# A modulation vector's columns: weighted sums on three engines, or one-column products on TensorE

## The chip, the core and the metric

The kernel runs on one core of a Trainium2 chip. Time is device time in microseconds (us) of one execution. Below, a "column" is one value for each of the 128 partitions.

## What is computed

Two transformer-like blocks follow one another on x of 1024 tokens by 1024 channels. Only the beginning of the first block matters here:

```python
mod = (jax.nn.silu(c) @ w_ada + b_ada)[:, None, :]      # c: (1, 1024), w_ada: (1024, 3072)
shift, scale, gate = jnp.split(mod, 3, axis=-1)
h = rms_norm(x, norm_g) * (1.0 + scale) + shift
... = jnp.split(h @ w_in, IN_OFFSETS, axis=-1)
```

All else (four attention-like branches on slices of `h @ w_in`, a merge, an output product scaled by `gate`, and the whole second block with its MLP) follows it. `p @ w_ple_proj` of the second block depends on inputs alone and is computed at the beginning as well.

## The kernel before, in words

Channels lie on partitions, in 8 pieces of 128 (KC = 8). Large products are made in three matmuls of 512 columns each, from a high and a low half of either operand (`mm3`, lines 229 to 231). A copy to the high half is line 147 (ScalarE) or 149 (VectorE); the subtraction that gives the low half is line 155 (GpSimd) or 157 (VectorE). Transposes are line 276.

The kernel is written in a framework that orders the instructions of each engine when it is compiled: by a priority, taken from the order of the program, and by a simulation of when operands are there. `stream(_T["STA"], -30000000)` gives the instructions traced inside it a priority ahead of all others, so that they are placed as soon as the simulation has them ready. `tc.issue_after(ins)` keeps instructions behind `ins` on the same engine. Each engine then runs its list strictly in that order.

The first stage, up to about 115 us, does this in the order of the program:

- It loads the rows of p and the weights of its projection, then the first half of x (512 tokens). All loads of this stage go through `load`, which puts them on SyncE's queue one behind the other.
- `proj(0)`, `x_norm(0)` and `proj(1)`: two halves of the projection of p (48 matmuls of 512 columns each), and between them the scaling and transposes of the first half of x.
- Four rounds over kp. Each makes two calls of `ada_cols` (one for 256 columns of the shift, one for 256 of the scale), then `x_mod(0, [kp])`, the modulation of two channel pieces: ScalarE makes the high half (line 412), VectorE the full value (line 413), VectorE or GpSimd the low half. Then come the first products with two pieces of K for four outputs (`first_products`, lines 506 to 508, 24 matmuls of 512 columns a round), which collect in four PSUM banks over all rounds.
- After that the second half of x is scaled, transposed and modulated (`x_norm(1)`), and the products of branch d go on. Then come sums for the gate (`ada_gate`), which have the same line numbers 455 and 458 but the tile name blk, and lie outside the question.

One call of `ada_cols` before: the 1024 by 256 weights come in two transfers of 512 KB (tile wada, eight buffers, 16 transfers in all). The 256 columns of eight pieces of K are multiplied by the piece's silu value (`sc`, one value a partition) and added up, elementwise: pieces 2, 3, 5, 6 and 7 on VectorE (one multiplication, line 455, four multiply-adds, line 458), pieces 0, 1 and 4 on ScalarE (line 451) with two additions on GpSimd (line 453). That leaves two tiles of 128 by 256 (adau). For each of its two outputs TensorE then adds these up over the partitions: the tile's 128 columns are loaded as weights, and a single column of ones is the moving operand (line 470), accumulated over the two tiles. A float32 product is two instructions of each kind in the trace, so 32 products show as 64. Lines 472 and 474 add the bias and form the scale on VectorE.

In the last round, 18 of the 24 products of the third round (outputs 1 to 3) are held behind the last column product by `issue_after`.

Of the kernel before, what the change touches and what calls it, by code (L numbers as in the profile page):

```python
# [9 lines left out]
F32 = mybir.dt.float32  # L10
F32R = mybir.dt.float32r
AF = mybir.ActivationFunctionType
ALU = mybir.AluOpType
# [4 lines left out]
P = 128  # L18
# [3 lines left out]
KC = D // P  # L22
# [54 lines left out]
def hybrid_then_mix_kernel(ctx: ExitStack, tc, I, c1, c2, out, dbg=None, upto=99):  # L77
    nc = tc.nc
    ve, ac, po, pe, sy = nc.vector, nc.scalar, nc.gpsimd, nc.tensor, nc.sync
# [9 lines left out]
    def nm(s):  # L89
        uid[0] += 1  # L90
        return f"{s}_{uid[0]}"

    def blk(dt=F32, shape=(P, 1024)):
        return main.tile(list(shape), dt, name=nm("blk"), tag="blk", bufs=NBLK)
# [10 lines left out]
    def mmb():  # L105
        return bank("mm", _T["MM"])
# [7 lines left out]
    def obk():  # L114
        return bank("o", _T["OB"])
# [87 lines left out]
    def kview(ap):  # L203
        return ap.rearrange("(k p) n -> p k n", p=P)
# [115 lines left out]
    start = ctx.enter_context(ExitStack())  # L320
# [6 lines left out]
    def load(dst, src):  # L327
        if prev[0] is None:
            d = sy.dma_start(dst, src)
        else:  # L330
            with tc.issue_after(prev[0].ins):
                d = sy.dma_start(dst, src)
        prev[0] = d
        return d
# [13 lines left out]
    def proj(half, early=False):  # L348
        if half not in pin:
            proj_load(half, sy.dma_start)  # L350
        b = pin[half]
        pT = A(2)
        pT.alloc(half, 0)
        for k in range(2):
            tp = trb()
            for q in range(4):
                transpose(tp[:, q * P:(q + 1) * P], b[:, q, k * P:(k + 1) * P], ident)
            copy(pT.hi(k, half), tp[:], "a")
            sub_lo(pT.lo(k, half), tp[:], pT.hi(k, half))
        for t in range(4 * half, 4 * half + 4):  # L360
            if early:
                proj_rows[t] = blk()
            for n in range(2):
                cs = slice(n * 512, (n + 1) * 512)
                m = mmb()
                gemm_N(m[:], pT, t, wproj[0], n * 512, n * 512 + 512)
                if early:
                    copy(proj_rows[t][:, cs], m[:], pick("pe", _T["PSE"]), 0.5)
                else:
                    o = tmp("acc", 512)  # L370
                    copy(o[:], m[:], "a", 0.5)
                    sy.dma_start(proj_d[t][:, cs], o[:])

    w_ada = kview(I["w_ada"][0])
# [9 lines left out]
    def x_norm(half):  # L384

        for t in range(4 * half, 4 * half + 4):
            xt = xin[t]
            ss = small(1)
            scr = cur[0].tile([P, 1024], F32, name=nm("scr"), tag="scr", bufs=1)
            sumsq(ss[:], xt[:], scr[:])  # L390
            r = small(1)
            rstd_of(r[:], ss[:], D, 1e-6)
            ve.tensor_scalar_mul(xt[:], xt[:], r[:, 0:1])
        for kp in range(4):
            xT[half, kp] = blk(F32, (P, 2, 512))
            if half:
                hT.alloc(half, kp)
            for j in range(2):
                k = 2 * kp + j
                tp = trb()  # L400
                for q in range(4):
                    transpose(tp[:, q * P:(q + 1) * P], xin[4 * half + q][:, k * P:(k + 1) * P], ident)
                if half:
                    x_mod1(half, kp, j, tp[:])
                else:
                    copy(xT[half, kp][:, j, :], tp[:], "a")
# [22 lines left out]
    sc = main.tile([P, 8], F32, name="sc", tag="sc", bufs=1)  # L429
# [4 lines left out]
    ones = main.tile([P, 1], F32, name="ones", tag="ones", bufs=1)  # L434
    ve.memset(ones[:], 1.0)
    aps = obk()
    mod = main.tile([P, 24], F32, name="mod", tag="mod", bufs=1)

    def ada(c0, n, new_u, new_w, dma, side=(), new_t=None):

        u, u2 = new_u(), side and new_u()
        per = 1024 // n
        fresh = True
        for k in range(KC):
            if k % per == 0:
                w = new_w()
                dma(w[:], w_ada[:, k:k + per, c0:c0 + n])
            wk = w[:, k % per, :]
            if k in side:
                t = u2 if k == min(side) else new_t()  # L450
                ac.activation(t, wk, AF.Copy, scale=sc[:, k:k + 1])
                if k > min(side):
                    po.tensor_tensor(u2, u2, t, op=ALU.add)
            elif fresh:
                ve.tensor_scalar_mul(u, wk, sc[:, k:k + 1])
                fresh = False
            else:
                ve.scalar_tensor_tensor(out=u, in0=wk, scalar=sc[:, k:k + 1], in1=u, op0=ALU.mult, op1=ALU.add)
        return [u, u2] if side else [u]

    def st_tile(tag, bufs, shape):
        return lambda: cur[0].tile([P] + shape, F32, name=nm(tag), tag=tag, bufs=bufs)[:]

    def ada_cols(c0):

        us = ada(c0, 256, st_tile("adau", 6, [256]), st_tile("wada", _T["WB"], [4, 256]), load, _T["PEA"], st_tile("adat", 2, [256]))
        c = slice(c0 // P, c0 // P + 2)
        for m in range(2):
            for j, u in enumerate(us):
                last = pe.matmul(aps[:, c.start + m:c.start + m + 1], u[:, m * P:(m + 1) * P], ones[:], start=(j == 0),  # L470
                                 stop=(j == len(us) - 1), skip_group_check=True)
        ve.tensor_add(mod[:, c], aps[:, c], V["b_ada"][:, c])
        if c0 >= 1024:
            ve.scalar_tensor_tensor(out=mod[:, c.start + 8:c.stop + 8], in0=mod[:, c], scalar=1.0,
                                    in1=V["norm_g"][:, c.start - 8:c.stop - 8], op0=ALU.add, op1=ALU.mult)
        return last
# [15 lines left out]
    def first_load(b):  # L492
        for q in range(2):
            w = wcols(2700 + 256 * q, order=(b,), dma=InOrder, hieng="a", loeng=_T["LW"])
            if b:
                first_w[q].h.update(w.h)
                first_w[q].l.update(w.l)
            else:
                first_w.append(w)

    def first_products(kp, qs):
        for q in qs:
            w, c = first_w[q // 2], q % 2 * P
            for k in (2 * kp, 2 * kp + 1):
                wh, wl, ah, al = w.hi(k, c, c + P), w.lo(k, c, c + P), hT.hi(k, 0), hT.lo(k, 0)
                pe.matmul(first_b[q][:], wh, ah, start=(k == 0), stop=False)
                pe.matmul(first_b[q][:], wh, al, start=False, stop=False)
                pe.matmul(first_b[q][:], wl, ah, start=False, stop=(k == 7))

    for kp in range(4):  # L510
        if kp in _T["FW"]:
            first_load(_T["FW"].index(kp))
        with stream(_T["STA"], -30000000):
            ada_cols(kp * 256)
        for c in _T["PO2"].get(kp, ""):
            if c == "x":
                x_norm(0)
            elif int(c) < _T["PS"]:
                proj(int(c), True)
        with stream(_T["STA"], -30000000):  # L520
            last = ada_cols(1024 + kp * 256)
            x_mod(0, [kp])
            if kp == 3 and _T["XN1"]:
                if _T["XL"] == 3:
                    x_load(1)
                x_norm(1)
        if kp + 10 in _T["FW"]:
            first_load(_T["FW"].index(kp + 10))
        if kp == 3:
            with tc.issue_after(last.ins):  # L530
                first_products(2, (1, 2, 3))
        first_products(kp, (0,) if kp == 2 else range(4))
        if kp == _T["XL"] and (kp < 3 or not _T["XN1"]):
            x_load(1)
    for t in proj_rows:
# [9 lines left out]
    def ada_gate():  # L545
        u = blk(F32, (P, 2, 512))
        for n in range(2):
            ada(2048 + n * 512, 512, lambda: u[:, n, :], lambda: blk(F32, (P, 2, 512)), sy.dma_start)
        gate_u.append(u)

    def ada_gate_sum():
# [792 lines left out]
    us, accs = [], [blk(), blk()]  # L1344
# [8 lines left out]
    for m in range(2):  # L1353
        u, w, evac = conf_group(m)
# [21 lines left out]
    qk0, w, evac = qk_group(0)  # L1376
# [367 lines left out]
    for g in LED:  # L1744
# [4 lines left out]
        w = load_w([(w_up[:, :, g * P:(g + 1) * P], 0)], P)  # L1749
# [241 lines left out]
    for stage in range(2):  # L1991
        ts = {}
        for i, (sn, tn) in enumerate(order):
# [5 lines left out]
            for q in range(4):  # L1999
# [18 lines left out]
                if (stage, i, q) in tails:  # L2018
                    t = tails[stage, i, q]
                    with tc.issue_after(split[q].ins):  # L2020
                        xn4[t] = finish_mlp(t)
                for c in range(2):
                    first, stop = q == 0 and c == 0, q == 3 and c == 1
                    for j in range(4):
# [4 lines left out]
                        last = pe.matmul(d, sl[:, c, ts_], th[:, c, :], start=False, stop=stop)  # L2029
# [48 lines left out]
    for t, j in todo:  # L2078
        c0, c1 = pieces(t)[j]
        m = mmb()  # L2080
        last = gemm_N(m[:, :c1 - c0], hg, t, w_ple[c0 // 512], c0 % 512, c0 % 512 + c1 - c0)
# [31 lines left out]
```

## Time and profile before

| | us |
|---|---|
| median of 3 runs (2320.02 to 2327.75) | 2320.87 |
| the profiled execution | 2326.91 |
| its span, first to last instruction | 2325.2 |
| TensorE busy in the span | 2239.4 |
| VectorE busy in the span | 1517.2 |
| ScalarE busy in the span | 966.2 |
| GpSimd busy in the span | 474.8 |

In the rows PE is TensorE, PEld its weight loads, DVE VectorE, ACT ScalarE, POOL GpSimd; SPq is the queue of SyncE. A name such as "o<-ones,adau" is output and inputs; L470 is the line. Matmuls are pipelined, so the duration of one includes time in which the next is already under way; what one takes of the engine's time is the distance between starts. Times in rows count from the first instruction of the profiled execution.

### The profile page before, as it was taken

The page shows a single profiled execution, that of the slowest core. Times are in us where ns is not written, and L with a number is a line of the kernel's source. Part 1 is how long each engine was busy: PE and PEld are TensorE (multiplying, and loading weights), DVE is VectorE, ACT ScalarE, POOL GpSimd, SP SyncE. Part 2 cuts the span into 40 slices and gives each one's busy share as a digit, 9 for nine tenths or more (in the row PEclk, how much of TensorE's full clock was granted, in tenths as well). Part 3 has the DMA queues.
Part 4 walks back from the last instruction along what each step waited for, and adds up shares of the span by engine and source line. Part 5 has one row for each costly group of instructions (what it writes and reads, how often), then busy time and mean ns, then how long its engine had stood idle before and what let it go on. Part 6 is the DMA issues. An engine that isn't in the chain of part 4 may idle for free.

```text
span 2325.2 us, 30286 instructions
## 1 busy us (share of the span) xinstructions
PE 2239.4 (96%) x11004; PEld 1860.3 (80%) x11004; DVE 1517.2 (65%) x2955; ACT 966.2 (42%) x1941; POOL 474.8 (20%) x404
## 2 busy tenths in 40 slices
PE   8999999999989999999998999899999999999998
PEld 6788888888877778877887787677788888888877
DVE  7634466665677965623579876866576678578684
ACT  6211344444455544422322344634545454344452
POOL 4222100010155622112330000012034340000021
PEclk8999999999999999999999999999999999999999
DMA  9421221121132333224221211156565687525313
GB/s 319 165 90 61 63 69 50 46 89 62 32 109 84 116 119 106 73 82 145 103 71 28 82 50 37 37 172 212 159 192 180 203 324 248 176 90 163 109 55 118
DMA packets 202783, 272.72 MB, mean 117 GB/s; under 512 B 17086, under 2 KB 126214, under 8 KB 202634
## 3 DMA queue, kind: packets, MB, share of 16 engines
q1 hardware_dynamic: 194240, 257.95, 34.3%
q10 hardware_dynamic: 8394, 12.84, 1.8%
q8 instruction: 87, 1.43, 0.3%
q14 instruction: 62, 0.51, 0.1%
HBM read 199.43 MB, written 71.32 MB: 116 GB/s over the span
## 4 chain that ended last, share of the span: by engine, by line
PE 82%; DVE 9%; DMA 3%; ACT 2%; POOL 2%; issue 2%; SPq 0%; POOLq 0%; DVEq 0%; ACTq 0%
PE mm L229 15%; PE mm L230 15%; PE mm L231 15%; PE t L276 4%; PE o L823 3%; DVE blk L1342 2%; PE s L1682 2%; PE s L1684 2%; PE s L1683 2%; PE t L2028 1%; PE t L2029 1%; PE t L2027 1%; PE mm L2028 1%; PE t L1682 1%; PE mm L2029 1%
## 5 line engine op out<-in xcount | busy, mean ns | idle before, releaser
L229 PE MATMUL mm<-blk,wh 128*128 128x512 f32 x1264 | 506.2, 401 | 20.8 <-DVE tz L1157 6.2
L230 PE MATMUL mm<-blk,wh 128*128 128x512 f32 x1264 | 500.6, 396 | 0.0
L231 PE MATMUL mm<-blk,wl 128*128 128x512 f32 x1264 | 499.1, 395 | 0.3 <-DVE wl L157 0.3
L229 PEld LDWEIGHTS mm<-blk,wh 128*128 128x128 f32 x1264 | 238.7, 189 | 74.3 <-DVE tz L1157 9.2
L231 PEld LDWEIGHTS mm<-blk,wl 128*128 128x128 f32 x1264 | 238.7, 189 | 50.4 <-DVE wl L157 0.8
L230 PEld LDWEIGHTS mm<-blk,wh 128*128 128x128 f32 x1264 | 239.0, 189 | 45.9
L229 PE MATMUL mm<-wh,blk 128*128 128x512 f32 (+3 forms) x544 | 199.2, 368 | 4.3 <-DVE blk L149 1.9
L155 POOL TENSOR_TENSOR wl<-wr,wh 128x1024 fp32r<-128x1024 f32 (+1 forms) x43 | 104.5, 2431 | 465.0 <-ACT wh L147 265.4
L231 PE MATMUL mm<-wh,blk 128*128 128x512 f32 (+3 forms) x544 | 195.9, 361 | 0.3 <-DVE blk L157 0.3
L157 DVE SCALAR_TENSOR_TENSOR wh<-blk,wh 128x1024 fp32r<-128x1024 f32 x116 | 138.4, 1219 | 67.7 <-issue 59.9
L147 ACT ACTIVATE wh<-blk 128x1024 fp32r<-128x1024 f32 x116 | 117.1, 1053 | 156.1 <-PE s L2028 86.1
L230 PE MATMUL mm<-wl,blk 128*128 128x512 f32 (+3 forms) x480 | 172.2, 359 | 6.6 <-DVE wl L157 6.5
L147 ACT ACTIVATE blk<-mm 64x512 fp32r<-64x512 f32 (+3 forms) x138 | 77.8, 569 | 175.6 <-PE mm L231 112.9
L147 ACT ACTIVATE PT<-t 128x512 fp32r<-128x512 f32 (+3 forms) x224 | 96.1, 459 | 116.9 <-PE o L823 70.7
L147 ACT ACTIVATE wh<-wr 128x1024 fp32r<-128x1024 f32 (+2 forms) x95 | 97.8, 1032 | 104.4 <-DMA wr<-in_w_in_dram 25.1
L157 DVE SCALAR_TENSOR_TENSOR PT<-t,PT 128x512 fp32r<-128x512 f32 (+3 forms) x224 | 110.7, 513 | 38.9 <-ACT PT L147 38.2
L309 POOL TENSOR_TENSOR sm<-sm,mhalf 128x1 f32<-128x1 f32 x64 | 38.5, 604 | 444.0 <-DVE sm L308 425.3
L157 DVE SCALAR_TENSOR_TENSOR wl<-wr,wh 128x1024 fp32r<-128x1024 f32 (+2 forms) x76 | 96.8, 1273 | 41.1 <-ACT wh L147 18.1
L229 PEld LDWEIGHTS mm<-wh,blk 128*128 128x128 f32 x544 | 105.6, 194 | 20.7 <-DVE blk L149 2.1
L231 PEld LDWEIGHTS mm<-wh,blk 128*128 128x128 f32 x544 | 104.9, 193 | 16.2 <-DVE blk L157 1.0
L230 PEld LDWEIGHTS mm<-wl,blk 128*128 128x128 f32 x480 | 93.9, 196 | 20.4 <-DVE wl L157 8.3
L1158 POOL TENSOR_TENSOR acc<-tz,acc 128x512 f32<-128x512 f32 x48 | 67.8, 1416 | 157.7 <-DVE tz L1157 119.8
(364 smaller groups left out, 4847.5 us busy)
## 6 DMA issues: line engine op xcount, KB each, us to landing
acc<-acc SPq DMA_DIRECT2D x96, 256.0 KB, 2.6
wr<-in_w_merge_dram SPq DMA_DIRECT2D x32, 512.0 KB, 3.7
wu<-in_w_up_dram SPq DMA_DIRECT2D x32, 512.0 KB, 5.1
blk<-in_w_down_dram SPq DMA_DIRECT2D x32, 512.0 KB, 7.0
blk<-ss SPq DMA_DIRECT2D x32, 512.0 KB, 4.6
wr<-in_w_in_dram SPq DMA_DIRECT2D x27, 512.0 KB, 4.5
ss<-us SPq DMA_DIRECT2D x48, 256.0 KB, 2.3
blk<-sa SPq DMA_DIRECT2D x24, 512.0 KB, 4.4
```

What stands on the lines that cost most here:

```text
L147: return ac.activation(dst, src, AF.Copy, scale=1.0 if scale is None else scale)
L155: return po.tensor_tensor(lo, x, hi.bitcast(F32), op=ALU.subtract)
L157: return ve.scalar_tensor_tensor(out=lo, in0=x, scalar=scale, in1=hi.bitcast(F32), op0=ALU.mult, op1=ALU.subtract)
L229: pe.matmul(dst, sh, mh, start=(i == 0), stop=False)
L230: pe.matmul(dst, sh, ml, start=False, stop=False)
L231: last = pe.matmul(dst, sl, mh, start=False, stop=(i == n - 1))
L276: pe.transpose(dst, src, ident)
L823: behind_pe[0] = pe.matmul(dst, v(lo + c0 + j), PT[:, j].rearrange("p a q -> p (a q)"), start=start and c0 + j == 0, stop=stop and c0 + j ...
L1158: po.tensor_tensor(acc[:], t[:], acc[:], op=ALU.add)
L1342: ve.scalar_tensor_tensor(out=acc[:, c:c1], in0=u[:, c - l:c1 - l], scalar=w, in1=acc[:, c:c1], op0=ALU.mult, op1=ALU.add)
L1682: pe.matmul(dst, wh, xh, start=first and k == 0, stop=False, skip_group_check=True)
L1683: pe.matmul(dst, wh, xl, start=False, stop=False, skip_group_check=True)
```

## The change

`ada_cols` no longer calls `ada`. It loads its two weight tiles and hands them to TensorE as they are: for each of its two outputs eight products, one for each piece of K, with the 128 by 128 weights stationary and the piece's column of `sc` as the only moving column, accumulated in PSUM. The multiplications and sums on VectorE, ScalarE and GpSimd, the tiles adau and adat and the product with ones are gone from it. `ada` remains for the gate alone, without the side engines. The first products of the third round are no longer split: all four outputs come in their own round.

```diff
--- before.py
+++ after.py
@@ -436,39 +436,32 @@
     aps = obk()
     mod = main.tile([P, 24], F32, name="mod", tag="mod", bufs=1)
 
-    def ada(c0, n, new_u, new_w, dma, side=(), new_t=None):
-
-        u, u2 = new_u(), side and new_u()
+    def ada(c0, n, u, new_w, dma):
+
         per = 1024 // n
-        fresh = True
         for k in range(KC):
             if k % per == 0:
                 w = new_w()
                 dma(w[:], w_ada[:, k:k + per, c0:c0 + n])
             wk = w[:, k % per, :]
-            if k in side:
-                t = u2 if k == min(side) else new_t()
-                ac.activation(t, wk, AF.Copy, scale=sc[:, k:k + 1])
-                if k > min(side):
-                    po.tensor_tensor(u2, u2, t, op=ALU.add)
-            elif fresh:
+            if k == 0:
                 ve.tensor_scalar_mul(u, wk, sc[:, k:k + 1])
-                fresh = False
             else:
                 ve.scalar_tensor_tensor(out=u, in0=wk, scalar=sc[:, k:k + 1], in1=u, op0=ALU.mult, op1=ALU.add)
-        return [u, u2] if side else [u]
 
     def st_tile(tag, bufs, shape):
         return lambda: cur[0].tile([P] + shape, F32, name=nm(tag), tag=tag, bufs=bufs)[:]
 
     def ada_cols(c0):
 
-        us = ada(c0, 256, st_tile("adau", 6, [256]), st_tile("wada", _T["WB"], [4, 256]), load, _T["PEA"], st_tile("adat", 2, [256]))
         c = slice(c0 // P, c0 // P + 2)
+        ws = [st_tile("wada", _T["WB"], [4, 256])() for _ in range(2)]
+        for b, w in enumerate(ws):
+            load(w, w_ada[:, 4 * b:4 * b + 4, c0:c0 + 256])
         for m in range(2):
-            for j, u in enumerate(us):
-                last = pe.matmul(aps[:, c.start + m:c.start + m + 1], u[:, m * P:(m + 1) * P], ones[:], start=(j == 0),
-                                 stop=(j == len(us) - 1), skip_group_check=True)
+            for k in range(KC):
+                last = pe.matmul(aps[:, c.start + m:c.start + m + 1], ws[k // 4][:, k % 4, m * P:(m + 1) * P], sc[:, k:k + 1],
+                                 start=(k == 0), stop=(k == KC - 1), skip_group_check=True)
         ve.tensor_add(mod[:, c], aps[:, c], V["b_ada"][:, c])
         if c0 >= 1024:
             ve.scalar_tensor_tensor(out=mod[:, c.start + 8:c.stop + 8], in0=mod[:, c], scalar=1.0,
@@ -526,10 +519,7 @@
                 x_norm(1)
         if kp + 10 in _T["FW"]:
             first_load(_T["FW"].index(kp + 10))
-        if kp == 3:
-            with tc.issue_after(last.ins):
-                first_products(2, (1, 2, 3))
-        first_products(kp, (0,) if kp == 2 else range(4))
+        first_products(kp, range(4))
         if kp == _T["XL"] and (kp < 3 or not _T["XN1"]):
             x_load(1)
     for t in proj_rows:
@@ -545,7 +535,7 @@
     def ada_gate():
         u = blk(F32, (P, 2, 512))
         for n in range(2):
-            ada(2048 + n * 512, 512, lambda: u[:, n, :], lambda: blk(F32, (P, 2, 512)), sy.dma_start)
+            ada(2048 + n * 512, 512, u[:, n, :], lambda: blk(F32, (P, 2, 512)), sy.dma_start)
         gate_u.append(u)
 
     def ada_gate_sum():
```

## Rows read from the trace of the kernel before

**Rows 1.** The page, busy us, share of the span, instructions of each engine.

```profile
PE 2239.4 (96%) x11004; PEld 1860.3 (80%) x11004; DVE 1517.2 (65%) x2955; ACT 966.2 (42%) x1941; POOL 474.8 (20%) x404
```

**Rows 2.** Stretches: length, busy of PE, PEld, DVE, ACT, POOL; clock; DMA share; GB/s.

```profile
26.20:30.80 4.60, 3.85 (x32) 3.39 (x32) 3.82 (x9) 4.60 (x11) 2.41 (x3) 1.00 1.09 348
30.80:37.60 6.80, 6.80 (x26) 5.88 (x26) 6.26 (x13) 5.14 (x11) 4.04 (x5) 0.52 1.09 349
...
48.30:51.30 3.00, 3.00 (x21) 2.42 (x19) 2.56 (x6) 3.00 (x7) 1.30 (x3) 1.00 0.91 318
51.30:58.10 6.80, 5.41 (x14) 4.24 (x14) 6.80 (x11) 4.16 (x8) 5.17 (x5) 0.52 1.01 345
58.10:78.30 20.20, 20.20 (x97) 16.80 (x96) 9.30 (x20) 6.03 (x11) 5.96 (x7) 0.99 0.36 147
...
82.00:85.40 3.40, 2.75 (x12) 2.33 (x11) 2.69 (x4) 2.57 (x4) 1.08 (x1) 0.54 0.67 195
```

**Rows 3.** Waits of TensorE, 20 to 100 us: total, times, longest.

```profile
PE mm L507 <- DVE blk L157: 1.4, 1, 1.4
PE t L276 <- DVE blk L393: 0.9, 1, 0.9
PE o L470 <- POOL adau L453: 0.7, 1, 0.7
PE mm L229 <- ACT blk L412: 0.7, 1, 0.7
```

**Rows 4.** Groups by line, TensorE, 22.5 to 78.3 us: count | busy, mean ns | idle before.

```profile
L229 PE MATMUL mm<-wh,blk 128*128 128x512 f32 x22 | 9.9, 449 | 0.0
...
L470 PE MATMUL o<-ones,adau 128*128 128x1 f32 x64 | 8.9, 252 | 0.7 <-POOL adau L453 0.7
L507 PE MATMUL mm<-blk,wh 128*128 128x512 f32 x16 | 7.2, 448 | 1.4 <-DVE blk L157 1.4
...
L276 PE MATMUL t<-c,blk 128*128 128x128 f32 x28 | 4.3, 307 | 0.0
```

**Rows 5.** Chain that ended last, 20 to 96 us: start, us taken in it, what.

```profile
22.27 0.23 PE mm L229
...
29.55 0.95 PE t L276 x8
...
32.33 1.07 PE o L470 x6
...
36.26 0.43 PE mm L229
...
48.46 0.80 PE o L470 x8
```

**Rows 6.** Groups by line, all engines, 20 to 70 us: columns as in rows 4.

```profile
L458 DVE SCALAR_TENSOR_TENSOR adau<-wada,sc,adau 128x256 f32<-128x256 f32 x32 | 25.7, 805 | 1.4 <-DMA wada<-in_w_ada_dram 0.6
L453 POOL TENSOR_TENSOR adau<-adau,adat 128x256 f32<-128x256 f32 x16 | 13.8, 868 | 5.2 <-ACT adat L451 4.3 <-PE o L470 0.7
```

**Rows 7.** The tile wada: min/median/max ns, first and last start in us.

```profile
L458 DVE SCALAR_TENSOR_TENSOR adau<-wada,sc,adau x32: 470/486/2707, 21.5 to 62.7; 128x256 f32<-128x256 f32 x32
L332 SPq DMA_DIRECT2D wada<-in_w_ada_dram x16: 1257/1418/2491, 11.0 to 38.9; - x16
...
DMA to landing us min/median/max: 8.5/9.2/9.9
```

**Rows 8.** Timelines of TensorE, ScalarE and GpSimd: start, us, what [idle before].

```profile
68.59 0.48 PE L506 MATMUL mm<-blk,wh 128*128 128x512 f32 x1
...
69.16 1.52 ACT L412 ACTIVATE blk<-blk,mod 128x512 fp32r<-128x512 f32 x2 [11.86 <-DVE mod L474]
70.59 1.05 ACT L312 ACTIVATE scr<-blk 128x1024 f32<-128x1024 f32 x1
...
71.83 1.30 POOL L155 TENSOR_TENSOR blk<-blk,blk 128x512 fp32r<-128x512 f32 x1 [9.40 <-DVE blk L413]
```

**Rows 9.** Timeline of TensorE, 100 to 121 us: columns as in rows 8.

```profile
112.84 0.47 PE L229 MATMUL mm<-wh,blk 128*128 128x268 f32 x1 [1.88 <-DVE blk L149]
```

## The prediction, made before the changed kernel was seen

> **What bounds the kernel now.** I read the page's busy shares first: TensorE is busy 96% of the span [rows 1]. That share alone says little about one stage, so I went to the stage that the change touches, the first 120 us. In the table of stretches [rows 2] TensorE is busy for all or nearly all of each stretch up to 78.3 us, and the waits of TensorE from 20 to 100 us [rows 3] add up to 3.7 us. So TensorE is already the engine that comes last in this stage, although VectorE, ScalarE and GpSimd make the modulation sums there. Busy is not the same as fast: the granted clock in [rows 2] is at its lower level (about 0.5, that is 1.2 of 2.4 GHz) from 30.8 to 37.6 and from 51.3 to 58.1 us.
>
> How much of that time is needed? From 22.5 to 78.3 us (55.8 us) the engine makes 66 matmuls of 512 columns for the projection (three lines of 22), 96 of 512 columns for the first products (six groups of 16), 28 transposes, and 64 instructions of one column, two for each of the 32 column products [rows 4]. What each takes out of the engine's time is read from the chain of waits, which has each instruction from its turn to the next one's: at the full clock 0.23 us for 512 columns, 0.95 / 8 = 0.119 us for a transpose, 0.80 / 8 = 0.100 us for one column with its weight load [rows 5]. That makes 162 x 0.23 + 28 x 0.119 + 64 x 0.100 = 37.3 + 3.3 + 6.4 = 47.0 us. The other 8.8 us of the 55.8 are waits and the half clock, and they are all that this stage can give back on TensorE.
>
> **What is removed.** In each of the eight modulation calls VectorE made five sums, ScalarE three scalings and GpSimd two additions. Four fifths of VectorE's took 25.7 us, GpSimd's 13.8 us [rows 6]. They lie beside TensorE's work. What they cost on the path is read from the wait rows: TensorE waited 0.7 us for a GpSimd addition and 1.4 us for a VectorE split that stood among the sums [rows 3]. There is a backlog behind the sums: the last weight transfer was issued at 38.9 us and took about 9.2 us to land, which is 48.1 us, yet the last sum starts at 62.7 us [rows 7]. The last columns could be ready some 14 us sooner. But TensorE doesn't stand idle for these 14 us; it makes the projection and the first products. Only the order of its work can change, so I credit the removal with the waits alone; they are within the 8.8 us.
>
> **What is added.** Each of 16 columns is now the sum of eight products instead of two: 128 products, 256 one-column instructions with a weight load each, 192 more. At the full clock this is 192 x 0.100 = 19.2 us, all on the engine that is last. At the lower level six such instructions took 1.07 us, 0.178 us each [rows 5]. So the 256 have the bounds 25.6 and 45.6 us.
>
> Which clock? One call now issues 32 of them in a row, 3.2 us at the full clock, and a call's 1 MB arrives every 3 us at the 348 GB/s of [rows 2], so for a while TensorE would do little else. In the trace the clock fell twice in this stage, both times right behind a stretch with many one-column products and transposes and few long matmuls: from 26.2 to 30.8 us, and from 48.3 to 51.3 us [rows 2]. From 58.1 to 78.3 us two bursts of eight stand between long rows of 512-column matmuls, and the clock stayed up [rows 2]. The new bursts are like the former two, so I take a third of the 256 at the full clock and two thirds at the lower: 85 x 0.100 + 171 x 0.178 = 38.9 us. Other matmuls caught between them run at half speed too, 0.43 us instead of 0.23 for 512 columns [rows 5]; I take 15 of them, 3 us, with bounds of 0 and 60 of them, 12 us.
>
> **What is moved.** Before, 18 matmuls of the first products (three outputs, third pair of K) were held back until the last column product had been issued. They start at 68.59 us, while ScalarE makes the high half of the modulated input from 69.16 us (two in 1.52 us) and GpSimd the last low half until 73.13 us [rows 8]. Afterwards they go in with their group and may be used up earlier. Then TensorE waits from 68.59 to the first high half at 69.92, 1.3 us, and at worst to the last low half, 4.5 us; if another product is left over, nothing. I take 2 us. In SP's queue nothing is added: the same 16 transfers in the same order. But their eight buffers are now released by TensorE, not by VectorE and ScalarE, and the rows of x and the stores of the projection stand behind the weights in that queue. The weights landed at 48.1 us, four transfers of x behind them are 2 MB, 6 us at the rate above, and ScalarE first reads them at 70.59 us [rows 8]; with some 16 us of slack a late release costs nothing by itself.
>
> **What is late next.** After 78.3 us TensorE transposes the second half of x. It waits 0.9 us for VectorE and 0.7 us for ScalarE there [rows 3], and from 82.0 to 85.4 us it is at the half clock, which costs half of 3.4 us [rows 2]. ScalarE's sums of squares of x stood in its order behind the modulation, and that waited for the columns [rows 8]; with TensorE later and the rest earlier these 3.3 us may go, and I credit them all. A wait of 1.88 us at 112.84 us [rows 9] belongs to the gate's sums and stays.
>
> **Sum.** Stage: 38.9 (columns) + 40.6 (projection, products, transposes) + 3 + 2 = 84.5 us against 55.8, so 28.7 us longer; less 3.3 is 25 us. Nothing behind this stage changes, so the end moves by as much. The profiled execution took 2326.91 us, 6 us above the median of 2320.87 and inside the three runs, so I put the difference on the median: **2346 us**.
>
> **The rivals.**
> (1) *The products keep their full-clock price.* Then the 25.6 us stand, and every wait and half-clock stretch of the stage goes: 25.6 + 40.6 = 66.2 us against 55.8, 10.4 longer, 12.4 if the wait of 2 us appears, less the 3.3 behind: +7 to +12 us, 2330 us. For it: most of the 64 instructions of before ran at the full price. Against it: the price at half clock, and the two falls named above.
> The Trainium skill bears on this one: "TensorE: Matmul & The Clock Gate", section "LDWEIGHTS (loading the stationary operand)", prices a weight load by its columns alone, 128 / 1.2 = 107 ns, whatever the clock. Estimated by the page, 192 more loads are 20.5 us at either level, which leads to this rival's time. The rows differ from it: 100 ns for load and product at the full clock and 178 ns at the lower [rows 5].
> (2) *It is absorbed (the other side).* TensorE's losses came from the sums: if all 8.8 us in the stage return, the 3.3 us behind it and the 1.88 us at 112.84 us as well, 14 of 19.2 us come back: +5 us, 2326 us. It decides from 12.2 us returned on, when under 7 us are left. For it: VectorE is rid of over 25 us of sums, and everything up to 113 us could start sooner. Against it: the wait rows name VectorE and GpSimd for little, and the half clock would have to vanish where one-column work is four times as much. To be faster than before it needs more than 19.2 us back, more than I can find.
> (3) *The columns are threaded through the other work and hold the clock down for all of it.* 45.6 us, 60 matmuls at half speed 12 us more, the wait at its 4.5: 45.6 + 40.6 + 12 + 4.5 = 102.7 against 55.8: 46.9 longer, less 3.3 is +44 us, 2365 us. For it: column calls become ready one by one as weights land, so the scheduler has reason to mix them with the projection. Against it: products that come in long rows brought the clock back within 7 us both times [rows 2].
>
> **How the numbers follow.** Forecast (2336 to 2358) 0.47; rival 1 (2327 to 2336) 0.20; rival 2 (2314 to 2327) 0.13, a small part of it below the time before; rival 3 (2358 to 2370) 0.20. About 0.3% (7 us) is what a measurement of this kernel can tell from no change. So faster has 0.03, the same 0.13 (rival 2 but for that part, and the lower edge of rival 1), slower 0.84. The range from 2326 to 2370 takes in rivals 1 and 3 and leaves out most of rival 2.
>
> **What would show it.** In the changed kernel's rows: 256 one-column instructions, each 0.10 us at the full clock and 0.18 at the lower; a granted clock near 0.5 over most of the stretch from about 25 us to the last column; the first products ending at 100 to 110 us instead of 78.3; VectorE, ScalarE and GpSimd with gaps before 60 us; the transposes of x's second half without the wait for VectorE. The prediction is wrong if the clock stays at its full level through the column products (rival 1), if the first products end before 88 us (rival 2), or if something behind 120 us changes by several us, which I have priced at nothing.

## The result, and the profile after

| | us |
|---|---|
| median before, four runs beside those of the change | 2321.22 |
| median after, four runs (2353.06 to 2358.56) | 2356.82 |
| ratio after to before, 95% interval | 1.0145 (1.0123 to 1.0168) |
| the profiled execution after | 2358.56 |
| its span | 2356.8 |

The change makes the kernel 35.6 us slower. The prediction was 2346 us, 25 us slower, with a range from 2326 to 2370.

Where the time lies is seen from marks that both kernels pass. The first stage ends with the last of the first products, followed by transposes of the second half of x. In the timeline of TensorE of the changed kernel (start, us, what) that is:

```profile
113.01 0.39 PE L501 MATMUL s<-blk,wl 128*128 128x512 f32 x1
113.25 1.47 PE L276 MATMUL t<-c,blk 128*128 128x128 f32 x12
```

Before, the same point was at 78.31 us, so the stage is 34.9 us longer:

```profile
78.31 0.81 PE L276 MATMUL t<-c,blk 128*128 128x128 f32 x6
```

Two later marks are the products of branch d with the tile Pm and the last transposes of Pm (minimum/median/maximum ns, first to last start in us), first in the kernel before, then after:

```profile
L721 PE MATMUL o<-blk,Pm x64: 217/275/277, 118.8 to 226.7; 128*128 128x64 f32 x64
L276 PE MATMUL t<-c,Pm x508: 270/272/473, 126.2 to 1505.6; 128*128 128x128 f32 x170
```

```profile
L711 PE MATMUL o<-blk,Pm x64: 217/275/275, 148.3 to 256.6; 128*128 128x64 f32 x64
L276 PE MATMUL t<-c,Pm x508: 270/272/476, 155.7 to 1534.8; 128*128 128x128 f32 x170
```

Of the 34.9 us, 5.4 are given back until the first product with Pm (118.8 to 148.3: 29.5 later). From there the shift stays within some 2 us: 29.2 us at the last transposes of Pm, 31.6 us at the end of the spans. The medians lie 35.6 us apart and the two profiled executions 31.6, because the profiled execution before was 5.7 us above the median of 2321.22 and the one after 1.7 us above its own.

The table of stretches of the changed kernel (length, then busy us and instructions of PE, PEld, DVE, ACT, POOL; granted clock; DMA share; GB/s) answers to [rows 2]:

```profile
22.50:27.00 4.50, 4.50 (x25) 3.81 (x25) 0.00 (x0) 3.54 (x7) 2.38 (x1) 1.00 1.09 348
27.00:31.00 4.00, 4.00 (x38) 3.96 (x37) 0.16 (x1) 1.32 (x4) 0.00 (x0) 1.00 1.09 348
31.00:37.00 6.00, 6.00 (x48) 6.00 (x47) 0.32 (x2) 2.17 (x5) 0.00 (x0) 0.81 1.09 347
37.00:47.00 10.00, 10.00 (x43) 9.52 (x43) 2.77 (x4) 3.08 (x4) 2.35 (x1) 0.50 0.51 165
47.00:54.00 7.00, 7.00 (x34) 6.91 (x34) 0.02 (x1) 0.00 (x0) 0.00 (x0) 0.50 0.24 71
54.00:63.20 9.20, 9.20 (x39) 8.62 (x39) 0.30 (x2) 1.19 (x2) 0.00 (x0) 0.50 0.97 325
63.20:68.50 5.30, 5.30 (x14) 4.14 (x15) 0.16 (x1) 0.60 (x1) 0.00 (x0) 0.50 1.02 417
68.50:72.00 3.50, 3.50 (x32) 3.50 (x30) 0.00 (x0) 0.60 (x1) 0.00 (x0) 0.94 0.68 279
72.00:75.60 3.60, 3.60 (x12) 2.82 (x11) 0.32 (x2) 0.60 (x1) 0.00 (x0) 0.54 0.00 0
75.60:79.00 3.40, 3.40 (x28) 3.24 (x26) 0.00 (x0) 0.60 (x1) 0.00 (x0) 0.98 0.25 100
79.00:92.50 13.50, 13.50 (x62) 11.82 (x63) 7.37 (x12) 5.30 (x8) 3.53 (x3) 0.63 0.28 93
92.50:113.20 20.70, 20.70 (x91) 16.97 (x90) 7.03 (x16) 7.21 (x12) 4.30 (x6) 0.99 0.20 54
```

TensorE is busy without a gap, VectorE and ScalarE have little to do until 79 us (4 and 14 us busy of 56.5), and the clock is at its lower level for some 34 us in one piece, from about 35 to 69 us, and again after that. Before, that level held twice for about 7 us in this stage. The chain of waits (start, us taken, what) gives the price of the column products (line 463 of the changed kernel) by call, as [rows 5] did before:

```profile
25.02 0.79 PE o L463 x8
...
27.30 2.57 PE o L463 x24
...
31.24 3.47 PE o L463 x32
...
37.19 6.62 PE o L463 x32
...
47.33 6.62 PE o L463 x32
...
56.71 6.62 PE o L463 x32
...
68.66 3.65 PE o L463 x32
...
76.74 4.31 PE o L463 x32
...
86.25 3.65 PE o L463 x32
```

The 256 instructions take 38.3 us. A call of 32 takes 3.5 to 3.7 us at the full clock (0.11 us each) and 6.62 us at the lower one (0.207 us each). The transfers were held up too: the tile wada's last transfer is now issued at 54.0 us instead of 38.9 [rows 7], because its buffer waits for TensorE (the fourth call, which reads that buffer before, ends at 47.33 + 6.62 = 53.95 us):

```profile
L332 SPq DMA_DIRECT2D wada<-in_w_ada_dram x16: 367/842/2849, 10.3 to 54.0; - x16
```

TensorE never waits for them; it is behind with what has landed.

### The profile page after: what moved, and what is told of

It is laid out like the page before. It is cut to its first block, busy times and chain, and to the rows that moved or that the text cites. A ratio compares the mean times of both kernels' runs of the same rounds, so it can differ in the third digit from the quotient of the medians.

```text
span 2356.8 us, 30562 instructions
## 1 busy us (share of the span) xinstructions
PE 2274.0 (96%) x11196; PEld 1891.3 (80%) x11196; DVE 1490.2 (63%) x2915; ACT 957.7 (41%) x1917; POOL 460.0 (20%) x388
## 4 chain that ended last, share of the span: by engine, by line
PE 82%; DVE 8%; DMA 3%; ACT 2%; POOL 2%; issue 2%; SPq 0%; DVEq 0%; POOLq 0%; ACTq 0%
PE mm L229 15%; PE mm L230 15%; PE mm L231 15%; PE t L276 4%; DVE blk L1332 3%; PE o L813 2%; PE s L1673 2%; PE s L1672 2%; PE s L1674 2%; PE o L463 2%; PE t L2018 1%; PE t L2019 1%; PE t L2017 1%; PE mm L2018 1%; PE t L1673 1%
## 5 line engine op out<-in xcount | busy, mean ns | idle before, releaser
L229 PE MATMUL mm<-wh,blk 128*128 128x512 f32 (+3 forms) x544 | 201.7, 373 | 4.2 <-DVE blk L157 1.3
L231 PE MATMUL mm<-wh,blk 128*128 128x512 f32 (+3 forms) x544 | 198.5, 366 | 0.3 <-DVE blk L157 0.3
L230 PEld LDWEIGHTS mm<-wl,blk 128*128 128x128 f32 x480 | 94.6, 197 | 22.3 <-DVE wl L157 8.8
```

Of the source, the lines that this page charges most:

```text
L229: pe.matmul(dst, sh, mh, start=(i == 0), stop=False)
L230: pe.matmul(dst, sh, ml, start=False, stop=False)
L231: last = pe.matmul(dst, sl, mh, start=False, stop=(i == n - 1))
```

## The experiments

The theory (A) going in: the loss is the price of the 192 added one-column instructions on the engine that was last already, doubled where the clock falls, and they are what makes it fall; the removal of the sums is worth no more than the stage's waits. Rivals: the removal itself costs or gains much (B, C), the half clock is owed to something else, the loss of the held-back products counts. All runs have their own runs of the kernel before on the same chip; medians of those were 2320.83 (first four), 2324.77 (next three) and 2324.39 us (the last). They differ by up to 4 us, so small differences between runs of different groups are better read from the ratios.

| run | median us | ratio to before, 95% interval |
|---|---|---|
| e_two | 2322.79 | 1.0008 (0.9998 to 1.0018) |
| e_both | 2360.65 | 1.0168 (1.0152 to 1.0183) |
| e_double | 2414.18 | 1.0406 (1.0390 to 1.0421) |
| e_wide | 2330.99 | 1.0043 (1.0029 to 1.0058) |
| e_four | 2323.89 | 0.9997 (0.9986 to 1.0008) |
| e_one | 2327.34 | 1.0016 (1.0007 to 1.0025) |
| e_bwide | 2325.15 | 1.0002 (0.9994 to 1.0011) |
| e_split | 2356.00 | 1.0136 (1.0119 to 1.0153) |

**The sums gone, the products not yet added.**

```diff
-            for k in range(KC):
+            for k in (0, 4):
...
```

> The changed kernel with two products a column instead of eight (pieces 0 and 4 of K; the other six pieces are left out of the modulation columns, so the time is that of a kernel which does less). TensorE has 64 one-column instructions, as many as the kernel before, and the sums on VectorE, ScalarE and GpSimd are gone: this isolates their removal. Theory A (the loss is the price of the 192 added instructions, the removal of the sums is worth little): 2312 to 2321 us, that is 0 to 9 us below the kernel before, and the first products end near 72 to 78 us. Theory B (the sums' removal itself, through a changed order or late buffers, costs time): clearly above the kernel before, 2330 us or more. Theory C (the sums were on the path and their removal is a real gain, hidden in the change by a larger loss): 2300 us or less.

The first products end at 70.15 us, and no clock loss is left in the stage (a half clock of 3.4 us comes later, in the 70s). The stretch row of its stage, and the point where it ends:

```profile
22.50:70.15 47.65, 47.47 (x257) 40.59 (x256) 14.46 (x32) 23.87 (x39) 11.02 (x8) 1.00 0.90 301
```

```profile
70.15 0.82 PE L276 MATMUL t<-c,blk 128*128 128x128 f32 x6
```

That is 47.65 us; 64 x 0.100 + 40.6 = 47.0 us was the prediction's sum for a stage without waits and half clock. So without the sums the 8.8 us of losses do go in this execution, as the prediction's sum assumed. The median of 2322.79 us is that of the kernel before within its interval, 2 us above what theory A expected and far from the 2330 and 2300 us of theories B and C, so both fall. The 8 us of the stage don't show in the median; the kernel before run again, below, bears on that.

**The sums kept, the instructions added.**

```diff
+        for m in range(2):
+            for k in (0, 1, 2, 4, 5, 6):
+                pe.matmul(aps[:, 32 + c.start + m:33 + c.start + m], ws[k // 4][:, k % 4, m * P:(m + 1) * P], sc[:, k:k + 1],
+                          start=(k == 0), stop=(k == 6), skip_group_check=True)
```

> The changed kernel with the sums of the kernel before restored and used (64 one-column instructions from them), and besides 192 one-column instructions on the weight tiles, whose results nobody reads: 256 in all, as in the changed kernel, and none of its relief on the other engines. Theory A (removal worth little): within 6 us of the changed kernel, 2351 to 2363 us. Theory C (removal is a real gain): above it by over 10 us, 2367 us or more. If less than 2345 us, the price isn't in the instructions.

2360.65 us is 39.8 us above its own runs of the kernel before, against 35.6 for the changed kernel: the whole loss appears with all of the old sums in place. What is added makes it, not what is removed. The stretch row of its stage, which ends at 108.91 us:

```profile
22.50:108.90 86.40, 86.40 (x449) 76.34 (x448) 44.13 (x78) 36.35 (x67) 25.52 (x26) 0.78 0.55 187
```

In the profiled executions the stage is 30.6 us longer than before and the span 34.9. The first product with Pm comes 24.8 us later (at 143.6 us), so 10 us of the loss arise behind it, where TensorE stands idle for 80.6 us instead of 70.8. Why isn't shown; this execution is the slowest of the four.

**Twice the products.**

```diff
-        for m in range(2):
+        for o, m in ((32, 0), (32, 1), (0, 0), (0, 1)):
             for k in range(KC):
...
```

> The changed kernel with each column product made twice, the second set into columns that nobody reads: 512 one-column instructions instead of 256. Theory A with half clock: the 256 more cost 0.15 us each as on average in the changed kernel (38.7 us for 256) up to 0.21 us as in its half-clock stretches, and some more matmuls run at half speed: 39 to 60 us more, 2396 to 2417 us. Rival (the instructions cost only their full-clock price and the half clock is owed to something else): 256 x 0.10 = 26 us more, 2383 us.

57 us more than the changed kernel. In the chain of waits a call of 64 takes 13.45 us, 0.210 us each, in four of the eight calls, and the nine entries of line 463 add up to 96.3 us, 58 more than in the changed kernel. The clock is at the lower level for 75 us in one piece, from about 30 to 105 us. The chain's rows of two calls, and the stretches:

```profile
39.19 13.45 PE o L463 x64
...
122.61 10.73 PE o L463 x64
```

```profile
27.00:102.00 75.00, 75.00 (x355) 73.80 (x354) 3.62 (x10) 7.86 (x13) 2.35 (x1) 0.52 0.46 152
102.00:172.70 70.70, 70.70 (x324) 63.19 (x325) 13.20 (x30) 15.01 (x24) 7.80 (x8) 0.71 0.14 46
```

At the full-clock price it would have been 26 us. The half clock belongs to these instructions, and more of them hold it down for longer.

**The same products, with 128 moving columns.**

```diff
+    scw = cur[0].tile([P, 8, P], F32, name="scw", tag="scw", bufs=1)
+    ve.memset(scw[:], 0.0)
+    ve.tensor_copy(scw[:, :, 0], sc[:])
...
-                last = pe.matmul(aps[:, c.start + m:c.start + m + 1], ws[k // 4][:, k % 4, m * P:(m + 1) * P], sc[:, k:k + 1],
+                last = pe.matmul(aps[:, (r0 + m) * P:(r0 + m + 1) * P], ws[k // 4][:, k % 4, m * P:(m + 1) * P], scw[:, k, :],
...
```

> The changed kernel with 128 moving columns in each product instead of one: the silu column and 127 columns of zeros, of which only the first result is used. Same count of instructions and weight loads. In the kernel before, transposes of 128 columns took 0.119 us and one-column products 0.100 us at the full clock, so the full-clock price hardly changes. Theory A (the clock falls because the array does next to nothing in one-column products): the half-clock time of the stage shrinks from 48 us to under 20, and the time falls to about 2330 to 2342 us. Rival (the clock falls for weight loads and small instructions of any width, or the pair costs more at any clock): half clock as long as in the changed kernel and 2357 to 2375 us.

2330.99 us is 10.2 us above its own runs of the kernel before: 25 of the 35.6 us are gone with 127 columns of zeros. Its stretches and the rows of the chain:

```profile
22.50:40.00 17.50, 17.50 (x138) 16.58 (x137) 1.94 (x5) 9.85 (x16) 2.38 (x1) 1.00 1.03 331
40.00:60.00 20.00, 20.00 (x144) 18.48 (x144) 2.02 (x8) 3.59 (x6) 2.40 (x1) 1.00 0.88 315
60.00:92.10 32.10, 32.10 (x174) 27.55 (x173) 14.33 (x27) 13.11 (x21) 7.88 (x8) 1.00 0.37 126
```

```profile
32.43 3.57 PE o L469 x32
...
66.71 3.57 PE o L469 x32
```

The granted clock is 1.00 throughout the stage. Every call of 32 takes 3.57 us, 0.112 us each, so 256 x 0.112 + 40.6 = 69.3 us; the stage measured 69.6. Both the count of instructions and of weight loads is that of the changed kernel, with no sums on VectorE in either. So the half clock goes with the single moving column: as many instructions and weight loads with 127 columns of zeros more don't have it. It alone is 21 us of the stage (90.75 against 69.6). Against before the stage is 13.8 us longer. That is the full-clock price less what the sums' removal gives back: 256 x 0.112 - 64 x 0.100 = 22.3 us, less the 8.8 us of losses, is 13.5.

**Half as many products.**

```diff
...
+                ve.tensor_scalar_mul(u, w[:, 2 * j, :], sc[:, k:k + 1])
+                ve.scalar_tensor_tensor(out=u, in0=w[:, 2 * j + 1, :], scalar=sc[:, k + 1:k + 2], in1=u, op0=ALU.mult, op1=ALU.add)
...
```

> The changed kernel with four products a column: VectorE adds the pieces of K in pairs (one multiplication and one multiply-add for each of four tiles a call), TensorE adds up the four tiles. 128 one-column instructions, bursts of 16. Theory A (price by number and clock): between the points measured, 64 instructions (2321 us) and 256 (2357 us): with the clock mostly up 64 x 0.10 = 6 us more than before, 2328 us; with half the stage at the lower clock 12 us more, 2333 us. A time like that of the changed kernel (over 2345 us) would mean that the loss doesn't follow the number of instructions.

The same time as before (ratio 0.9997), where 6 to 12 us more were expected. The first products end at 77.19 us, the granted clock is 0.97 over the stage, and no engine but VectorE makes sums:

```profile
22.50:77.20 54.70, 54.70 (x315) 47.59 (x314) 40.23 (x97) 25.11 (x42) 12.99 (x10) 0.97 0.85 289
```

128 x 0.100 + 40.6 = 53.4 us against 54.7 measured. Before, the stage took 55.8 us for half as many instructions, because it had 8.8 us of waits and half clock; most of these are gone here, and that pays for the 64 more. The loss doesn't grow evenly with the number: from 64 instructions (e_two) to 128 the stage grows by 7 us, from 128 to 256 by 36.

**Fewer still, and the kernel before with wide products.**

```diff
+        po.tensor_tensor(us[1], us[1], us[0], op=ALU.add)
+        us = us[1:]
```

> The kernel before with the two tiles of sums of each call added by GpSimd, and one product a column: 32 one-column instructions instead of 64, at the price of eight more additions on GpSimd (0.87 us each). Theory A: 32 x 0.10 = 3 us less, and bursts half as long, so perhaps less of the half clock, up to 6 us less: 2312 to 2318 us. Rival (the column chain of sums bounds the stage): 0 to 7 us more, 2321 to 2328 us.

```diff
-                last = pe.matmul(aps[:, c.start + m:c.start + m + 1], u[:, m * P:(m + 1) * P], ones[:], start=(j == 0),
+                last = pe.matmul(aps[:, (r0 + m) * P:(r0 + m + 1) * P], u[:, m * P:(m + 1) * P], ones[:].to_broadcast([P, P]), start=(j == 0),
```

> The kernel before with 128 moving columns of ones in each column product instead of one (the same column read 128 times); sums and split order as before. Theory A (one-column products let the clock fall): the half-clock stretches of the first stage (30.8 to 37.6 and 51.3 to 58.1 us, together worth up to 7 us) go or shrink, at 64 x 0.012 = 1 us for the wider products: 2314 to 2319 us. Rival (those two stretches come from waits and transposes): no change, 2321 us.

Theory A expected both to be faster. Neither beats the kernel before in the median: e_one is 0.16% slower, within what the rival expected, and e_bwide takes the same time. The stretch rows of their stages, e_one first:

```profile
22.50:76.70 54.20, 47.70 (x221) 37.29 (x221) 42.40 (x71) 33.89 (x66) 33.30 (x33) 0.97 0.80 269
```

```profile
22.50:74.40 51.90, 49.07 (x253) 40.19 (x252) 40.87 (x71) 33.65 (x65) 26.43 (x25) 1.00 0.82 278
```

In e_one TensorE stands idle for 6.5 of the 54.2 us: with fewer products to make, it waits for the sums. In e_bwide it is idle for 2.8 of 51.9 us, little more than before (2.1 of 55.8). With wide products the clock stays at 1.00 in the kernel before as well. That fits the view that its two falls were owed to one-column products, but doesn't show it: e_two, with the same 64 one-column instructions, had no fall in its stage either.

e_two, e_four, e_one and e_bwide pass the first product with Pm 9.1, 6.4, 5.7 and 6.7 us ahead of the profiled execution before, and their spans are 6.2, 2.5, 4.2 and 4.7 us shorter than its span. Yet none of their medians is clearly below that of the kernel before.

**The kernel before again.**

> The kernel before, unchanged, once more with a profile, to see where executions of one kernel differ from one another after the first stage. Both theories: the first 120 us agree within 0.5 us with the profile shown; the end differs by up to 6 us.

The expectation for the first 120 us was wrong: this execution ends its first products 1.4 us earlier than the other one and passes the first product with Pm 3.6 us earlier, in the same code:

```profile
76.94 0.82 PE L276 MATMUL t<-c,blk 128*128 128x128 f32 x6
```

```profile
L721 PE MATMUL o<-blk,Pm x64: 217/275/275, 115.2 to 223.1; 128*128 128x64 f32 x64
```

Its clock is up from 31 to 38 us, where the other one's was at the lower level [rows 2]:

```profile
31.00:38.00 7.00, 5.90 (x35) 4.67 (x34) 6.89 (x14) 5.32 (x12) 3.53 (x5) 1.00 1.09 348
38.00:51.00 13.00, 11.78 (x62) 9.77 (x61) 11.65 (x18) 10.92 (x22) 7.45 (x7) 0.97 1.02 317
51.00:58.20 7.20, 7.03 (x19) 5.55 (x20) 7.20 (x14) 2.92 (x6) 4.90 (x5) 0.58 1.01 375
```

So of the 6 to 9 us named above, 3.6 lie within what an unchanged kernel does from one execution to the next. The comparison also flatters the variants: the profiled execution before lies 5.7 us above the median, and those of e_one and e_bwide are the fastest of their 12 and 11 runs. The part of the kernel behind the first product with Pm takes part of the lead back. In rows from that product to the end of the span (kernel before, before again, e_two, e_both) TensorE is busy for the same time, within 2 us, and idle for 70.8, 74.3, 74.9 and 80.6 us:

```profile
118.80:2325.20 2206.40, 2135.56 (x10515) 1774.96 (x10513) 1439.09 (x2821) 909.58 (x1841) 432.83 (x361) 0.99 0.35 111
115.20:2324.10 2208.90, 2134.60 (x10515) 1774.00 (x10513) 1436.44 (x2821) 909.81 (x1841) 433.47 (x361) 0.99 0.35 111
109.70:2319.00 2209.30, 2134.39 (x10515) 1774.16 (x10513) 1436.24 (x2821) 908.54 (x1841) 434.87 (x361) 0.99 0.35 111
143.60:2360.10 2216.50, 2135.95 (x10515) 1772.77 (x10513) 1430.01 (x2821) 908.16 (x1841) 434.09 (x361) 0.99 0.34 110
```

The unchanged kernel loses 2.5 us of its lead of 3.6 in this way. So these traces don't tell a gain of a few us in the first stage from no gain; the changed kernel's and e_double's losses come through whole.

**The held-back products put back.**

```diff
+        if kp == 3:
+            with tc.issue_after(last.ins):
+                first_products(2, (1, 2, 3))
-        first_products(kp, range(4))
+        first_products(kp, (0,) if kp == 2 else range(4))
```

> The changed kernel with the 18 products of the third round held behind the last column product again, as in the kernel before: the third part of the change undone by itself. In the changed kernel TensorE waits 0.4 us in the whole stage, so there is no gap for them to cover. Theory A: within 4 us of the changed kernel, 2352 to 2361 us. The prediction's term (2 us, at most 4.5, for lost cover): 2 to 5 us less than the changed kernel, 2352 to 2355 us, with a wait of TensorE behind the last column product in the changed kernel that goes here. A larger gain, under 2350 us, would mean that the split does something else, for example keeps the clock up by long matmuls between the last columns.

The median is 0.8 us less than the changed kernel's; against their own runs of the kernel before, the loss is 31.6 us here and 35.6 there, with ratios whose intervals overlap. In its profiled execution the first products end at 106.47 us instead of 113.25, with the lower clock for 34 us of the stage instead of 48:

```profile
22.50:106.40 83.90, 83.90 (x444) 74.83 (x443) 18.45 (x39) 25.77 (x42) 12.57 (x10) 0.80 0.57 192
```

This is the fastest of its four executions, and the profiled one of the changed kernel is the slowest of its four, so I don't put the 6.8 us down to the split; that it saves a few us through the clock isn't excluded. TensorE waits for nothing in either stage, so there was no gap to cover.

## Why the prediction was right

The direction, the mechanism and its place were right: TensorE was last before, the added instructions are all on it, and the clock falls behind them. The median of 2356.82 us lies at the upper edge of the forecast's own band (2336 to 2358). Of the signs, two came out larger than stated: the first products end at 113.25 us, not at 100 to 110, and an instruction at the lower clock takes 0.207 us, not 0.18. Term by term, against the profiled execution after:

- **The column products** were put at 38.9 us and took 38.3. Two errors cancel in that, so its closeness is luck. The price at the lower clock was taken from six instructions [rows 5] at 0.178 us; over whole calls it is 0.207 in the changed kernel and 0.210 in e_double, twice the full-clock price. And 96 of the 256 ran wholly at that price, where I had taken two thirds; the other 160 took 18.4 us, 0.115 each, most of them at the full clock.
- **Matmuls caught at half speed** were put at 3 us, with 12 as the bound. This is the term that was mis-sized. The stage took 90.75 us, of which 38.3 are columns and 40.6 the projection, products and transposes at the full clock; 11.8 are left, and TensorE doesn't wait, so they are the half clock on other work. The timeline shows why: the scheduler set 6 to 12 projection matmuls between two calls, and some 50 of them, and of the first products, ran at the lower clock, where 15 were predicted. Their starts lie 0.43 us apart (first rows below). This was a part of rival 3, whose bound of 12 us it reached.
- **Lost cover** of 2 us: nothing. TensorE reached the point so late that all its operands were there; it waits for nothing in the stage, in e_split as little as in the changed kernel.
- **The sums' removal** was credited with the stage's 8.8 us of waits and half clock, in that the stage was summed without them. e_two shows this for one execution: 47.65 us for a sum of 47.0.
- **Behind the stage** 3.3 us were credited and 5.4 came back. From the end of the stage to the first product with Pm (second rows below, before and after) TensorE is busy 3.4 us less, as the clock is at 1.00, and idle 2.1 us less. The wait for ScalarE is gone and that for VectorE is 0.2 us, as the prediction had it. What it didn't credit is a second half-clock stretch of 3.4 us before, at 113 us, and 0.8 us of the wait of 1.88 us [rows 9], which it expected to stay and which is 1.1 us now. The kernel before run again has no half clock at 113 us either, so that part may be chance.
- **Sum**: the stage became 34.9 us longer where 28.7 was predicted: 31.9 more for the columns (38.3 less the 6.4 of before) and 11.8 on the other work, less the 8.8. That is nearly all of the miss in the profiled executions, 31.6 us against 25.4. Behind the first product with Pm, priced at nothing, 2.1 us were added (31.6 against 29.5), less than the waits there differ between two executions of the kernel before (70.8 and 74.3 us). The sum was made against an execution 6 us above the median and then put on the median, which is where most of the rest of the distance to the 35.6 us of the medians lies. Whether the usual execution before has less half clock in its first stage isn't shown.

Rows for the second term, from the timeline of TensorE in the changed kernel (start, us, what), and for the fifth, the stretches between the two marks before and after:

```profile
63.76 0.63 PE L230 MATMUL mm<-wl,blk 128*128 128x512 f32 x1
64.19 0.63 PE L231 MATMUL mm<-wh,blk 128*128 128x512 f32 x1
```

```profile
78.31:118.80 40.49, 36.88 (x188) 30.98 (x186) 27.76 (x46) 10.38 (x16) 10.81 (x9) 0.92 0.52 165
113.25:148.30 35.05, 33.53 (x188) 28.16 (x186) 27.38 (x39) 9.33 (x14) 10.32 (x8) 1.00 0.44 144
```

Rival 1 is refuted by the changed kernel's rows at half clock, and e_wide is what it would have looked like: 10.2 us more than before, for +7 to +12 in its working (whose upper end leaves out the 3.3 us; with them it is +9). The page it leaned on, the Trainium skill's "TensorE: Matmul & The Clock Gate", section "LDWEIGHTS (loading the stationary operand)", gives one price of 107 ns for a load of 128 columns. That agrees roughly with the 0.100 to 0.112 us that load and product take together at the full clock here, and not with the 0.207 us at the lower one: the measurement decides. Rival 2 had its mechanism in part (the losses of the stage do go with the sums in e_two's trace), but the added work is 43.7 us (31.9 and 11.8) where it allowed for 19.2. Rival 3 was right in that other work is held down, and wrong in that all 256 products would pay the lower clock.

## What to carry to other kernels

Where TensorE is last in a stage, moving elementwise sums from an idler engine to one-column products on it adds their weight loads to the path, and a stretch made of them can take the clock from all matmuls set in between: cost the neighbours too, not only the products. If such products must be made in numbers, look at the granted clock of their stretch; here 127 further moving columns of zeros cost about 0.01 us an instruction (0.112 against 0.100) and gave back 25 us. And a gain of a few us in an early stage, read from one trace against another, is not yet a gain: four variants were 6 to 9 us ahead after some 120 us, of which 3.6 are within what the unchanged kernel does, and no median was clearly lower.

## What was not expected of the hardware

- TensorE fully busy, with its weight loads busy 9.5 of 10 us, stayed at half clock for 34 us of one-column products with matmuls of 512 columns between them (changed kernel), and for 75 us with twice as many products (e_double); with 128 columns for each of these loads it stayed at the full clock for the whole stage (e_wide).
- At the lower clock the pair of weight load and one-column product takes 0.207 us, twice its price at the full one; a matmul of 512 columns takes 0.43 us instead of 0.23.
- Two executions of the same kernel can differ by a whole half-clock stretch of 7 us. They were 1.4 us apart at the end of the first stage and 3.6 us at the first product with Pm (kernel before and before_again).
